# Layer 0's output projection in pairs of tiles by seven half-size block products, with the residual by accumulating DMAs, in a two-layer backbone

## The chip, the cores and the metric

The kernel runs on one core of one Trainium2 chip. The metric is the device time of one execution in microseconds (us). The engines are called PE (TensorE, matmuls), PEld (TensorE's weight load, which overlaps PE), DVE (VectorE), ACT (ScalarE), POOL (GpSimd) and SP (SyncE, which here issues DMAs only). Each of them works through its own queue of instructions in order; DMAs can be issued from SP, ACT and POOL. L1940 means line 1940 of the kernel before.

## The reference

A backbone of two layers over 2304 tokens (256 of a context, 2048 latent), 1024 wide. Each layer normalizes, modulates by a condition, mixes, projects, gates and adds the residual:

```python
for i in range(DEPTH):                       # DEPTH = 2
    shift, scale, gate = modulation(c, ada_w[i], ada_b[i])
    c_shift, c_scale, c_gate = modulation(c_ctx, ada_w[i], ada_b[i])
    h = rms_norm(x, norm_g[i]) * (1 + scale) + shift
    hc = rms_norm(cx, norm_g[i]) * (1 + c_scale) + c_shift
    if i % 2 == 0:
        y, yc = even_mixer(h, hc, ...)       # latent attention and gated linear attention, then @ ev_w_out
    else:
        y, yc = odd_mixer(h, hc, ...)        # neighbourhood attention, then @ od_w_out
    x = x + gate * y
    if update_ctx:                           # layer 0 only
        cx = cx + c_gate * yc
return x
```

What the change touches is the end of each layer. Layer 0: `x1 = xin + gate0 * (R @ w_out0)`, where `R` (2304x1024, kept transposed in device memory as `RT`) is the mixer's gated output, `w_out0` is 1024x1024, and the first two tiles of tokens, the context, take another gate vector. Layer 1: `out = x1 + gate1 * ((RT1 * z1) @ w_out1)` for the latent tokens alone, where `z1` is the mixer's own gate.

## The kernel before, in words

The tokens are 18 tiles of 128. All matmuls are single-precision by three products: each operand is split into a high part (a rounding, done by ACT at L106) and a low part (the difference, done by DVE), and `hi*hi + hi*lo + lo*hi` is accumulated in PSUM (L108 to L131; L129, L130 and L131 are the three).

The program is built under a scheduler that simulates the engines: it decides the order of the instructions in each engine's queue, and hoists an instruction as far as its inputs and its place in memory let it. `issue_after(x)` holds an instruction behind `x`. Buffers come from pools of named tiles; a load into a tile waits until its last user is done.

Stages, with their times in the profiled execution:

- *Constants, modulation and the latent products* (0 to 545 us). `ada_first` (L255, L258) multiplies the 8 MB of layer 0's modulation weights `ada_w` by the condition; `transposed` (L326) loads a tile, normalizes it (squares on ACT, the reciprocal root by `rpow`, L208 and L210, on POOL, the scaling at L336 on DVE) and transposes it on PE (L339, tile `px`); `modulate` makes `hhi` and `hlo` from it. Tile 0's `transposed` stands ahead of `ada_first`.
- *The rest of layer 0's input products*, `even_rest` (L607; 545 to 1095 us), cell by cell: for a tile and a column block, matmuls, an activation, and a store by a DMA from POOL (L635 to L639).
- *Mixing*, `even_mix` (L1164; 1095 to 1895 us): attention and the gated linear attention woven together; in it the 16 chunks of `w_out0` are split into high and low parts as room comes free (`unit`, L1210 ff.), and tile 0's load and split for the projection are made early.
- *Layer 0's output*, `project` (L1296; 1895 to 2093 us). For each of the 18 tiles: `project_load` (L1258) loads the tile of `RT` (`pr`, 512 KB) and the residual tile of the input (`px`, 512 KB) on SP; `project_split` (L1266; ACT L106, DVE L1268) makes its parts `prh` and `prl`; `project_steps` (L1270) runs two halves of 512 columns, each 8 blocks of k by three matmuls into a PSUM bank `pj`, multiplies a half by the gate into `py` (DVE, L1284), adds the residual (POOL, L1288) and stores the tile to `x1` (SP, L1290). 48 matmuls per tile, 864 in all. After each tile a step of `ahead()` runs: splits of layer 1's weight blocks `w_od` j = 2 and 3, and the preparation of layer 1's tiles 0 and 1 from `x1`.
- *Layer 1's input products*, `odd_qk` and `odd_vz` (2093 to 3010 us). The copies of `x1` into the output (L1455, 16 of 512 KB, ACT's queue, device memory to device memory) belong to `odd_vz` in the source; the scheduler has them at 1942 to 2098 us, each after the store of its tile.
- *Layer 1's attention and output* (3010 to 3567 us). The output is already done the new way: four plain tiles, then six pairs of tiles. A pair is a 2x2 block product (rows: two tiles; k and columns: halves of 512) by seven products of half size, 12 matmuls each, 84 in all, where two plain tiles take 96 (`seven`, L1920 ff.; the matmuls at L1940). It needs sums and differences of the weight blocks once (`weight_sums`, L1847), of the operands per pair (`operands`, L1910), copies of three partial results by ACT, and final sums and gates on DVE (L1950 ff.). The results are added to the output by accumulating DMAs from POOL (L1286 for plain tiles, L1960 for pairs, 256 KB each). The product with `z1` (`product`, L1808, 128x1024 elements) runs on POOL.

Of the kernel before, what the change touches and what calls it, by code (L numbers as in the profile page):

```python
# [17 lines left out]
P = 128  # L18
# [70 lines left out]
class Kern:  # L89
# [236 lines left out]
    def transposed(self, t, src, pp, tag, xp=None):  # L326

        nc, sp = self.nc, self.prp
        x = self.tl(xp or sp, [P, D], "x", bufs=1)
# [71 lines left out]
    def even_latent(self, ws, wrest, kept):  # L401
# [6 lines left out]
        with ExitStack() as es:  # L408
# [3 lines left out]
            with ExitStack() as es2:  # L412
                st = self.pool(es2, "adaS", side="left", reuse_waits="tile")
                rows = self.transposed(0, self.i["xin"], pp, px, st)
# [192 lines left out]
    def even_rest(self, ws, win, hT):  # L607
        nc = self.nc
        self.zaT = self.scr("zaT", (4, P, T), F32)
        with ExitStack() as es:  # L610
# [5 lines left out]
            def cell(t, j):  # L616
# [547 lines left out]
    def even_mix(self, e1, win, hT):  # L1164
        nc = self.nc
        self.RT = self.scr("RT", (KD, P, T), F32)
        self.x1 = self.scr("x1", (T, D), F32)
        with ExitStack() as es:
            with ExitStack() as esa:
# [31 lines left out]
                def side():  # L1201
# [11 lines left out]
                    pre[0] = self.project_load(self.RT, 0, self.i["xin"], ld)  # L1213
                    yield "unit"
                    yield "unit"
                    r, x = pre[0]
                    hi, lo = self.tl(ld, [P, KD, P], "prh", F32R, bufs=1), self.tl(ld, [P, KD, P], "px", F32R)
                    self.project_split(r[:], hi[:], lo[:])
                    pre[0] = hi, lo, r, x
# [9 lines left out]
            def ahead():  # L1229
                for j in (2, 3):  # L1230
                    yield from self.od_steps(win, j, ws)
                for t in range(2):
                    hT[t] = self.prep(1, t, self.x1, pp, ("pj", 4))
                    yield
                    yield

            u = 2 * KD - 1
            self.split_unit(w, u, self.load_unit(u, self.tl(sp, [P, 512], "py")), [self.tl(g1, [P, 512], "gG", F32R, bufs=2)[:] for _ in range(2)])
            gate = [self.gate_load(0, c, self.tl(sp, [P, D], f"gate{c}", bufs=1)[:]) for c in range(2)]
            self.project(self.RT, range(NT), self.i["xin"], self.x1, w, sp, pp, pre["ld"], pre, gate, ahead())  # L1240
# [17 lines left out]
    def project_load(self, RT, t, xsrc, ld):  # L1258
# [3 lines left out]
        x = self.tl(ld, [P, D], "px")  # L1262
        self.nc.sync.dma_start(x[:], xsrc[t * P : t * P + P, :])
        return r, x
# [26 lines left out]

    def gate_load(self, l, c, g):
# [3 lines left out]
    def project(self, RT, tiles, xsrc, dst, w, sp, pp, ld, pre, gate, ahead):  # L1296

        for t in tiles:
            if t in pre:
                hi, lo, r, x = pre.pop(t)  # L1300
            else:
                hi, lo = [self.tl(sp, [P, KD, P], "pr" + c, F32R)[:] for c in "hl"]
                r, x = self.project_load(RT, t, xsrc, ld)
                self.project_split(r[:], hi, lo)
            for _ in self.project_steps(hi, lo, x, gate[1 if t < NCT else 0], w, lambda: self.tl(pp, [P, 512], "pj", bufs=4),
                                        lambda: self.tl(sp, [P, 512], "py"), dst[t * P : t * P + P, :]):
                pass
            next(ahead, None)


# [212 lines left out]
    def odd_attention(self, out, right, left, wout):  # L1523
# [4 lines left out]
        with ExitStack() as es:  # L1528
# [278 lines left out]
            def product(z, r):  # L1807
                nc.gpsimd.tensor_tensor(out=r[:], in0=r[:], in1=z[:], op=ALU.mult)  # L1808
# [20 lines left out]
            PLAIN = 4  # L1829
            h4 = KD // 2  # L1830
            half = [slice(0, 512), slice(512, D)]
            by_k = lambda x: x.rearrange("p (k t) -> p k t", t=P)
            T1, T2, T3, T4 = [], [], [], [[x[:, 0, :] for x in wout[k, 1]] for k in range(h4)]
            B = lambda k0, n: [[x[:, 0, :] for x in wout[k, n]] for k in range(k0, k0 + h4)]

            def room():

                for dst, i in ((T1, 1), (T2, 0)):
                    q = [qtile(9, i, 1), qtile(9, i, 2)]
                    dst.extend([x[:, k * 512 : k * 512 + 512] for x in q] for k in range(h4))  # L1840
                v = self.tl(vp[1], [P, NT, P], "ov", F32R, bufs=1)[:].rearrange("p t d -> p (t d)")
                tb = [self.tl(tp[1], [P, NR, NC], f"tab{i}", F32R, bufs=1)[:].rearrange("p r c -> p (r c)") for i in range(2)]
                T3.extend([v[:, k * 512 : k * 512 + 512], tb[k // 2][:, k % 2 * 512 : k % 2 * 512 + 512]] for k in range(h4))

            def weight_sums():

                dif = lambda e, o, x, y: e.tensor_tensor(out=o, in0=x, in1=y, op=ALU.subtract)  # L1847
# [6 lines left out]
                room()  # L1854
                for k in range(h4):
                    u, v = [(low[i][:, half[0]], low[i][:, half[1]]) for i in (k, k + h4)]
                    dif(nc.vector, u[0], u[1], u[0])
                    self.project_split(u[0], *T1[k])
                    dif(nc.vector, u[1], v[1], u[1])
                    dif(nc.vector, v[1], v[1], u[0])  # L1860
                    self.project_split(v[1], *T2[k])
                    yield
                    dif(nc.vector, v[0], v[0], v[1])
                    self.project_split(u[1], *T3[k])
                    if k == h4 - 1:
                        late_sums.extend((low[i][:, half[0]], T4[i - h4]) for i in range(h4, KD))
                    yield

            late_sums = []
            sums_w = weight_sums()  # L1870
# [16 lines left out]
            def whole(x):  # L1887
                return by_k(x[:].rearrange("p i c -> p (i c)"))
# [4 lines left out]

            hA = [whole(self.tl(kp, [P, 2, 512], "kt1", F32R, bufs=2)) for _ in range(2)]
            h4w = whole(ones["kt"][1])
            hS4 = [h4w[:, :h4, :], h4w[:, h4:, :]]
            hS, hB = two(1), two(0)
            first4, last4 = slice(0, h4), slice(h4, KD)

            def pair_load(t):  # L1900

                za, ra = tile(t)
                zb, rb = tile(t + 1)
                product(za, ra)
                product(zb, rb)
                return za, ra, zb, rb

            def operands(za, ra, zb, rb):

                tt = lambda o, x, y, op: nc.vector.tensor_tensor(out=o, in0=x, in1=y, op=op)  # L1910

                def sums():
                    tt(za[:, first4, :], rb[:, first4, :], rb[:, last4, :], ALU.add)
                    tt(za[:, last4, :], za[:, first4, :], ra[:, first4, :], ALU.subtract)
                    self.project_split(za[:], *hS)

                def more():
                    tt(rb[:, first4, :], ra[:, first4, :], rb[:, first4, :], ALU.subtract)
                    tt(zb[:, first4, :], ra[:, last4, :], za[:, last4, :], ALU.subtract)
                    self.project_split(zb[:, first4, :], *hS4)  # L1920

                return [lambda: self.project_split(ra[:], *hA), sums, more, lambda: self.project_split(rb[:], *hB)]

            def seven(t):

                nonlocal mm, done
                end = t + 2 == NT - NCT
                if end:
                    res = exps([P, 512])
                    self.load(res[:], self.x1[CTX + (t + 1) * P : CTX + (t + 2) * P, :512])  # L1930
                U = self.tl(pp, [P, 8, 64], "o", bufs=4)[:].rearrange("p r c -> p (r c)")
                V, W = bank()[:], bank()[:]
                tile_of = lambda h, n: [x[:, n * h4 : n * h4 + h4, :] for x in h]

                def prod(ps, A, Bk, start):
                    nonlocal mm
                    with self.tc.issue_after(mm.ins) if mm else ExitStack():
                        for k in range(h4):
                            for n, (x, y) in enumerate(((A[0], Bk[k][0]), (A[0], Bk[k][1]), (A[1], Bk[k][0]))):
                                mm = nc.tensor.matmul(ps, x[:, k, :], y, start=start and k == 0 and n == 0, stop=k == h4 - 1 and n == 2,  # L1940
                                                      skip_group_check=True)

                def copy(ps, pool, tag, bufs):
                    x = self.tl(pool, [P, 512], tag, bufs=bufs)
# [158 lines left out]
```

## Time and profile before

| | us |
|---|---|
| median of 3 runs | 3563.45 (3563.01 to 3563.81) |
| profiled execution, its own time | 3569.04 |
| span of its trace | 3567.2 |
| PE busy in the span | 3465.4 (97%) |
| DVE, ACT, POOL busy | 2400.1, 1419.3, 1248.8 |
| mean granted clock of PE | 0.987 |

The span is the profiled execution's trace from its first to its last record; the 1.8 us around it are not in the trace. The *table of stretches* gives busy time by engine in chosen windows of the span; the *chain* follows the work that ended last back from the end, from each piece to what released it; a *timeline* lists one engine's instructions in order of start, with the idle time ahead of each and what ended it in brackets; a view *by tile* or *by line* lists the instructions that touch a tensor or stand on a line, as minimum, median and maximum duration. Busy time is no measure of what a stage costs: what matters is which engine is never idle in that stage, or which wait ends last.

### The profile page before, as it was taken

To read this page: it belongs to the slowest core of one execution; us is meant where nothing else is said; L and a number is where in the kernel's file an instruction comes from. 1 tells how busy PE (TensorE), PEld (TensorE's weight loads), DVE (VectorE), ACT (ScalarE), POOL (GpSimd) and SP (SyncE) were. 2 spreads that over 40 slices of the span, in tenths; PEclk is the share of its full clock that TensorE was granted. 3 is DMA by queue.
4 is the path that set the end of the run, shared out by engine and by line. 5 is a ranking of instruction groups with operands and counts; after the bars stand their busy time and mean duration, and the time that the engine had idled before them with its cause. 6 is when DMAs were issued, how large, how long until landed. Compare 5 with 4: busy or idle time off the path is not lost.

```text
span 3567.2 us, 54003 instructions
## 1 busy us (share of the span) xinstructions
PE 3465.4 (97%) x19532; PEld 2680.1 (75%) x19532; DVE 2400.1 (67%) x4709; ACT 1419.3 (40%) x2562; POOL 1248.8 (35%) x1382
## 2 busy tenths in 40 slices
PE   7999998999999999999999999999899999999999
PEld 6888987888896666665557878888788887555577
DVE  4677655888885777768874345545577784666775
ACT  5454552111113455446653124444422223555532
POOL 1333431100101333322212233333334443888842
PEclk9999999999999999999999999999999999999999
DMA  7555554222215242334526654445744447888675
GB/s 252 150 155 161 148 144 137 72 87 76 86 52 153 64 132 79 110 111 139 169 82 210 212 174 134 139 144 167 234 146 127 145 121 189 214 218 223 188 213 92
DMA packets 377292, 521.52 MB, mean 146 GB/s; under 512 B 34153, under 2 KB 253753, under 8 KB 370866
## 3 DMA queue, kind: packets, MB, share of 16 engines
q1 hardware_dynamic: 329762, 418.42, 40.7%
q0 software_dynamic: 24096, 63.26, 6.8%
q10 hardware_dynamic: 23168, 36.38, 2.9%
q8 instruction: 155, 2.54, 0.3%
q14 instruction: 111, 0.91, 0.1%
HBM read 338.62 MB, written 187.69 MB: 148 GB/s over the span
## 4 chain that ended last, share of the span: by engine, by line
PE 80%; DMA 7%; DVE 6%; ACT 2%; POOL 2%; issue 2%; SPq 1%; DVEq 0%; ACTq 0%; POOLq 0%
PE st L1130 10%; PE gm L129 10%; PE gm L130 10%; PE gm L131 10%; PE av L1040 7%; PE mx L660 4%; PE o L1624 2%; PE st L1590 2%; DMA wraw<-w_od 2%; PE pj L129 2%; PE pj L131 2%; PE pj L130 2%; PE o L1940 2%; DMA adaw<-ada_w 1%; PE st L1940 1%
## 5 line engine op out<-in xcount | busy, mean ns | idle before, releaser
L661 DVE TENSOR_REDUCE mm<-mx 128x1 f32<-128x512 f32 (+1 forms) x656 | 388.6, 629 | 82.3 <-PE mx L660 75.2
L106 ACT ACTIVATE apt<-st 128x1024 f32<-128x1024 f32 (+1 forms) x296 | 300.2, 1015 | 308.6 <-PE st L1130 293.7
L1137 DVE TENSOR_TENSOR acc<-acc,apt 128x1024 f32<-128x1024 f32 x256 | 340.6, 1330 | 81.0 <-ACT apt L106 61.6
L1130 PE MATMUL st<-aq,akh 64*128 64x512 f32 x1728 | 313.9, 410 | 1.1 <-ACT apt L106 0.8
L1040 PE MATMUL av<-apt,av 128*64 128x512 f32 x1152 | 265.8, 598 | 0.0
L1749 DVE TENSOR_TENSOR opt<-st,tab 128x64 f32<-128x64 f32 (+10 forms) x576 | 144.5, 318 | 144.3 <-PE st L1591 66.4
L660 PE MATMUL mx<-mk,mq 96*128 96x512 f32 (+1 forms) x656 | 236.0, 373 | 2.1 <-DMA mq<-QC 1.4
L1630 POOL TENSOR_TENSOR oacc<-oacc,opt 128x576 f32<-128x576 f32 (+5 forms) x192 | 223.3, 1190 | 38.5 <-DVE oacc L1614 13.8
L1130 PE MATMUL st<-aq,akl 64*128 64x512 f32 (+1 forms) x1152 | 231.8, 392 | 0.0
L1130 PEld LDWEIGHTS st<-aq,akh 64*128 64x128 f32 x1728 | 154.1, 186 | 83.0 <-ACT apt L106 29.1
L106 ACT ACTIVATE u<-gm 128x352 f32<-128x352 f32 (+1 forms) x140 | 68.5, 497 | 368.3 <-PE gm L131 208.3
L1507 DVE CUSTOM_DVE_ANT_1 mx<-mx,mtab 128x217 f32<-128x217 f32 (+12 forms) x576 | 184.0, 338 | 37.5 <-PE mx L1501 28.2
L1040 PEld LDWEIGHTS av<-apt,av 128*64 128x64 f32 x1152 | 76.3, 136 | 135.2 <-issue 134.2
L106 ACT ACTIVATE opt<-opt 128x930 f32<-128x930 f32 (+8 forms) x130 | 104.4, 805 | 110.0 <-DVE opt L1749 106.4
L660 PEld LDWEIGHTS mx<-mk,mq 96*128 96x128 f32 x656 | 121.2, 188 | 14.9 <-DVE mm L661 1.9
L1130 PEld LDWEIGHTS st<-aq,akl 64*128 64x128 f32 (+1 forms) x1152 | 113.0, 185 | 23.1
L106 ACT ACTIVATE x<-px,modB,modA 128x128 f32<-128x128 f32 x272 | 99.5, 468 | 59.5 <-PE px L339 56.5
L129 PE MATMUL gm<-w1h,hhi 128*128 128x512 f32 x288 | 116.2, 404 | 6.9 <-ACT onat L106 6.9
L129 PE MATMUL gm<-w0h,hhi 128*128 128x512 f32 x288 | 116.5, 404 | 1.9 <-DVE hhi L351 1.9
L130 PE MATMUL gm<-w1l,hhi 128*128 128x512 f32 x288 | 115.1, 400 | 0.0
L210 POOL TENSOR_TENSOR oss<-oss,mhalf 128x8 f32<-128x8 f32 x68 | 113.2, 1665 | 5.1
L130 PE MATMUL gm<-w0l,hhi 128*128 128x512 f32 x288 | 114.6, 398 | 0.0
(579 smaller groups left out, 9700.9 us busy)
## 6 DMA issues: line engine op xcount, KB each, us to landing
q<-Q SPq DMA_DIRECT2D x48, 512.0 KB
H<-x ACTq DMA_DIRECT2D x36, 512.0 KB
adaw<-ada_w SPq DMA_DIRECT2D x64, 256.0 KB
x<-H SPq DMA_DIRECT2D x32, 512.0 KB
wraw<-w_od SPq DMA_DIRECT2D x64, 256.0 KB
K1t<-okt POOLq DMA_DIRECT2D x32, 512.0 KB, 7.3
kt<-K1t SPq DMA_DIRECT2D x32, 512.0 KB
mtab<-rpb_q SPq DMA_DIRECT2D x16, 899.0 KB
```

Of the source, the lines that this page charges most:

```text
L106: return self.nc.scalar.activation(out, in_, func, **kw)
L129: self.nc.tensor.matmul(out, lh(k), rh(k), start=start and j == 0, stop=False)
L130: self.nc.tensor.matmul(out, lh(k), rl(k), start=False, stop=False)
L131: yield self.nc.tensor.matmul(out, ll(k), rh(k), start=False, stop=stop and j == n - 1)
L660: mm = nc.tensor.matmul(ps[:, :w], q[:A_QK, (t % 6) * P : (t % 6) * P + P], k[:A_QK, k0 : k0 + w], start=True, stop=True)
L661: nc.vector.tensor_reduce(out=m[:, t, n : n + 1], in_=ps[:, :w], axis=AX.X, op=ALU.max)
L1040: mm = nc.tensor.matmul(O[j, nb][i * 64 : i * 64 + 64, :w], V[j, kt // TT][:, kt % TT, i * 64 : i * 64 + 64], pts[:, i, :w], start=n == 0, ...
L1130: mm = nc.tensor.matmul(ps[:, o // 64, :w], k[o : o + r, kb, kq], Q[o : o + r, qb, :w], start=m == 0, stop=m == 4)
L1137: added = nc.vector.tensor_tensor(out=acc[:, :, :w], in0=a[:, :, :w], in1=pts[:, :, :w], op=ALU.add)
L1507: nc.vector.tensor_tensor_reduce(out=s, in0=s, in1=tb[:, ri : ri + rn, ci : ci + cn], scale=1.0, scalar=-3e38, op0=ALU.add, op1=ALU.max, a ...
L1630: self.psum = nc.gpsimd.tensor_tensor(out=a, in0=a, in1=pts[:, :, a0 - r0 : a1 - r0, :], op=ALU.add)
L1749: bias = nc.vector.tensor_tensor(out=pt[:, d[0], d[1]], in0=ps[:, d[0], d[1]], in1=tabs[j][i][:, ri : ri + rn, ci : ci + cn], op=ALU.add)
```

## The change

1. Layer 0's output: tiles 0 to 3 stay plain; tiles 4 to 17 are taken in seven pairs, each by seven block products (780 matmuls in all instead of 864). The code of layer 1's pairs becomes shared methods (`weight_sums`, `pair_operands`, `seven`, `pair_result`).
2. The residual: in `even_rest`, behind the cell j = 1 of each tile, a DMA from POOL copies the tile of the input to `x1`, in device memory (18 of 512 KB). The results are added to `x1` by accumulating DMAs from POOL of 256 KB (two per plain tile, four per pair: 36). The loads of `px`, POOL's adds and the stores of `x1` go.
3. The rest of the weight sums' operands are loaded as whole rows of `w_out0` (8 of 512 KB on SP) at the stage's start, and the sums are made during the plain tiles.
4. The splits of `w_od` j = 2 move into the pairs, those of j = 3 to the end of the last pair (their place holds two weight sums until then); layer 1's tiles 0 and 1 are prepared inside the last pair.
5. Layer 1's product with `z1` moves from POOL to DVE.

The core of the diff:

```diff
 def even_rest(self, ws, win, hT):
+    self.x1 = self.scr("x1", (T, D), F32)
...
             elif j == 1:
                 nc.gpsimd.dma_start(self.Un[t, :, 1056:], u[:])
+                nc.gpsimd.dma_start(self.x1[t * P : t * P + P, :], self.i["xin"][t * P : t * P + P, :])
...
 def even_mix(self, e1, win, hT):
-    self.x1 = self.scr("x1", (T, D), F32)
...
-        self.project(self.RT, range(NT), self.i["xin"], self.x1, w, sp, pp, pre["ld"], pre, gate, ahead())
+        self.even_output(w, sp, pp, pre, win, hT, ws)
...
+    def seven(self, h, w, U, V, W, copy, result):
...
+        prod(U, part(h["A"], 0), w["B11"], True)
+        s1 = copy(U, 0)
+        prod(V, part(h["S"], 0), w["T1"], True)
+        s5 = copy(V, 1)
+        prod(U, part(h["S"], 1), w["T2"], False)
+        u2 = copy(U, 2)
+        prod(W, part(h["A"], 1), w["B21"], True)
+        self.done = result(W, s1, 0, 0)
+        yield
+        prod(U, part(h["B"], 0), w["T3"], False)
+        self.done = result(U, s5, 1, 1)
+        yield
+        prod(V, h["S4"], w["B22"], False)
+        self.done = result(V, u2, 0, 1)
+        yield
+        prod(U, part(h["B"], 1), w["T4"], False)
+        self.done = result(U, None, 1, 0)
+        yield
...
+    def even_output(self, w, sp, pp, pre, win, hT, ws):
...
+        def weights7():
+            raw = [self.tl(ws[0], [P, h4, D], "w0" + z, bufs=1) for z in "hl"]
+            for k in range(h4):
+                for n, x in enumerate(raw):
+                    nc.sync.dma_start(x[:, k, :], self.i["w_out0"][:, n * h4 + k, :])
...
+            for k in range(h4):
+                yield from self.weight_sums(raw[0][:, k, :], raw[1][:, k, :], *(w7[t][k] for t in ("T1", "T2", "T3")))
+            late.extend((raw[1][:, k, self.HALF[0]], w7["T4"][k]) for k in range(h4))
...
+        def result(t):
+            def f(ps, x, row, n):
+                x, done = self.pair_result(ps, x, gates[0][:, self.HALF[n]], y)
+                nc.gpsimd.dma_start(self.x1[(t + row) * P : (t + row) * P + P, self.HALF[n]], x[:], accum_op=ALU.add)
+                return done
+            return f
...
+        ahead = self.od_steps(win, 2, ws)
+        for t in range(PLAIN, NT, 2):
+            end = t + 2 == NT
+            if not end:
+                ops = pair(t + 2)
+            U = self.tl(pp, [P, 512], "pu", bufs=2)
+            for n, _ in enumerate(self.seven(h7, w7, U[:], bank()[:], bank()[:], copy, result(t))):
+                if not end:
+                    with self.tc.issue_after(self.done.ins):
+                        ops[n]()
+                    if n == 3:
+                        next(ahead, None)
+                elif n < 2:
+                    xp = None if n == 0 else (ld, "pr")
+                    hT[n] = self.modulate(1, n, *self.transposed(n, self.x1, pp, ("pj", 4), xp))
+        for _ in ahead:
+            pass
+        for _ in self.od_steps(win, 3, ws):
+            pass
...
             def product(z, r):
-                nc.gpsimd.tensor_tensor(out=r[:], in0=r[:], in1=z[:], op=ALU.mult)
+                nc.vector.tensor_tensor(out=r[:], in0=r[:], in1=z[:], op=ALU.mult)
```

More of the change, by code (lines that the diff above doesn't have):

```diff
@@ L1299, in project @@
             if t in pre:
[L1300 removed]
+                hi, lo = pre.pop(t)
             else:
[L1302 to L1307, printed above, removed]
@@ L1308, in project @@
-            next(ahead, None)
+                hi, lo = parts()
+                self.project_split(self.project_load(self.RT, t, ld)[:], hi, lo)
+            if t == 0:
+                next(sums)
+            for n, _ in enumerate(self.project_steps(hi, lo, None, gates[1 if t < NCT else 0], w, bank, y, self.x1[t * P : t * P + P, :])):
+                if t and n % 5 == 4:
+                    next(sums, None)
+        for _ in sums:
+            pass
+        s4 = self.tl(ld, [P, KD, P], "prh", F32R, bufs=1)
@@ new lines, in even_output @@
+        ops, self.mm = pair(PLAIN), None
+        for n in range(4):
+            ops[n]()
+            if n == 1:
+                for x, place in late:
+                    self.project_split(x, *place)
+        ahead = self.od_steps(win, 2, ws)
[7 more added lines that the diff above has]
+                    with self.tc.issue_after(self.done.ins):
+                        ops[n]()
+                    if n == 3:
[3 more added lines that the diff above has]
+                    hT[n] = self.modulate(1, n, *self.transposed(n, self.x1, pp, ("pj", 4), xp))
@@ L1892, in two @@
                 return [by_k(x[:, i].rearrange("p r c -> p (r c)")) for i in range(2)]
[L1894 to L1903, printed above, removed]
+            s4 = whole(ones["kt"][1])
@@ L1904, in pair_load, with pair @@
+            h7 = {"A": [whole(self.tl(kp, [P, 2, 512], "kt1", F32R, bufs=2)) for _ in range(2)], "S": two(1), "B": two(0),
+                  "S4": [s4[:, :h4, :], s4[:, h4:, :]]}
+            def pair(t):
+                (za, ra), (zb, rb) = [tile(t + n) for n in range(2)]
                 product(za, ra)
                 product(zb, rb)
[L1906 to L1922, printed above, removed]
@@ L1981, in odd_attention, with copy, result, f @@
-            after = pair_load(PLAIN)
-            ops, done = operands(*after), None
+                return self.pair_operands(ra[:], rb[:], za[:], h7)
+            def copy(ps, n):
+                x = self.tl(fp, [P, 512], "rc", bufs=3) if n == 2 else self.tl(lp, [P, 512], "rl", bufs=2)
+                self.act(x[:], ps)
+                return x
+            def result(t, res):
+                def f(ps, x, row, n):
+                    add = x is None and res
+                    x, done = self.pair_result(ps, x, gate[:, self.HALF[n]], y)
+                    dst = out[(t + row) * P : (t + row) * P + P, self.HALF[n]]
+                    if add:
+                        nc.vector.tensor_tensor(out=x[:], in0=x[:], in1=res[:], op=ALU.add)
+                        nc.sync.dma_start(dst, x[:])
+                    else:
+                        nc.gpsimd.dma_start(dst, x[:], accum_op=ALU.add)
+                    return done
+                return f
@@ L1988, in odd_attention @@
             for t in range(PLAIN, NT - NCT, 2):
-                if t + 2 < NT - NCT:
-                    after = pair_load(t + 2)
-                    ops = operands(*after)
-                for n, _ in enumerate(seven(t)):
-                    if t + 2 < NT - NCT:
-                        with self.tc.issue_after(done.ins):
+                end = t + 2 == NT - NCT
+                if not end:
+                    ops = pair(t + 2)
+                else:
+                    res = exps([P, 512])
+                    self.load(res[:], self.x1[CTX + (t + 1) * P : CTX + (t + 2) * P, :512])
+                U = self.tl(pp, [P, 8, 64], "o", bufs=4)[:].rearrange("p r c -> p (r c)")
+                for n, _ in enumerate(self.seven(h7, w7, U, bank()[:], bank()[:], copy, result(t, res))):
+                    if not end:
+                        with self.tc.issue_after(self.done.ins):
                             ops[n]()
```

194 lines of the change are left out of this document (92 added, 102 removed).

## The prediction

> **What bounds the kernel now.** I read the page first (busy time, slices, chain), then the table of stretches stage by stage, then the timelines of the engines in the stretches that the change touches.
>
> ```profile
> span 3567.2 us, 54003 instructions
> PE 3465.4 (97%) x19532; PEld 2680.1 (75%) x19532; DVE 2400.1 (67%) x4709; ACT 1419.3 (40%) x2562; POOL 1248.8 (35%) x1382
> PE 80%; DMA 7%; DVE 6%; ACT 2%; POOL 2%; issue 2%; SPq 1%; DVEq 0%; ACTq 0%; POOLq 0%
> 0.00:5.00 5.00, 0.00 (x0) 0.00 (x0) 0.69 (x4) 1.50 (x2) 1.40 (x12) 1.00 0.41 121
> 10.00:15.00 5.00, 4.68 (x18) 1.48 (x16) 0.00 (x0) 0.00 (x0) 0.00 (x0) 1.00 1.00 424
> 25.00:30.00 5.00, 4.24 (x24) 2.03 (x24) 1.29 (x3) 1.77 (x4) 0.00 (x0) 1.00 1.01 396
> 40.00:100.00 60.00, 49.35 (x282) 46.13 (x282) 38.18 (x56) 30.61 (x67) 10.99 (x18) 0.94 0.60 186
> 100.00:545.00 445.00, 428.30 (x2570) 394.71 (x2570) 305.21 (x574) 229.10 (x538) 167.41 (x307) 0.99 0.56 151
> 1970.00:2090.00 120.00, 120.00 (x538) 99.45 (x538) 43.47 (x41) 17.35 (x28) 29.97 (x24) 1.00 0.58 195
> ```
>
> TensorE (PE) is busy 97% of the span and is 80% of the chain, so a matmul that goes is worth its time wherever PE is full. The rows of stretches give, after the length, the busy time of PE, PEld, DVE, ACT and POOL, then granted clock, DMA share and GB/s. Layer 0's output (1895 to 2093 us) is a stage in which PE is never idle and the other engines are under half busy. The start is the opposite: from 10 to 30 us the sixteen DMA engines are full (share 1.00, about 424 GB/s).
>
> **The change, part by part.** All sums are differences, first against the profiled execution (3569.04 us, span 3567.2), which is 5.59 above the median of the runs, 3563.45; I add the sum to the median.
>
> *1. The products.* Seven pairs take 84 matmuls where two plain tiles take 96.
>
> ```profile
> 2009.74 0.39 PE L129 MATMUL pj<-D,prh 128*128 128x512 f32 x1
> 2009.97 0.39 PE L130 MATMUL pj<-D,prh 128*128 128x512 f32 x1
> 1955.35 0.69 DVE L1284 TENSOR_TENSOR py<-pj,gate 128x512 f32<-128x512 f32 x1 [2.02 <-PE pj L131]
> 1960.79 0.69 DVE L1284 TENSOR_TENSOR py<-pj,gate 128x512 f32<-128x512 f32 x1 [4.75 <-PE pj L131]
> 3484.16 2.79 PE st L1940 x12
> 3503.62 2.79 PE st L1940 x12
> 3523.08 2.79 PE st L1940 x12
> 3542.54 2.79 PE st L1940 x12
> ```
>
> A half tile (24 matmuls) ends every 5.44 us by the DVE rows, 0.227 per matmul; two tiles are 4 x 5.44 = 21.76 us. A pair by seven products exists in layer 1: the chain's rows repeat every 19.46 us. At the plain pitch it would be 84 x 0.2267 = 19.04. So a pair saves 2.30 to 2.72, seven pairs **16.1 to 19.0 us; I take 17.5**, between the two because this stage ran at clock 1.00, layer 1's at 0.98. Weight sums (28 DVE operations of 128x512, 0.69 each, 19 us) and T4's splits lie beside the four plain tiles (44 us, in which DVE is a third busy); the loads of tiles 1 to 3 stand ahead of the 4 MB of weights on SP, so none of it costs PE time. POOL's adds and the stores were not on the path: nothing is gained from them.
>
> *2. The residual copies.* In the source they stand in the second stage (545 to 1095 us). But nothing that they read is produced by the kernel, and in the built program's order for POOL all 18 stand at the very start, right behind the constants: eight without a wait, the next eight each waiting for the copy eight before it, then the first half of tile 0's root-mean-square (L208), then copies 17 and 18 (waiting for 9 and 10), then its second half (L210). Two things are queued behind a wait there: tile 0's normalization, and through it every first product. And 9.44 MB travel in the stretch whose DMA engines are full.
>
> ```profile
> 4.51 15.89 DMA adaw<-ada_w
> 27.14 3.61 PE gm L258 x16
> 35.39 0.94 PE L120 MATMUL gm<-W0h,hhi 128*128 128x352 f32 x2
> 2087.08 0.50 ACTq L1455 DMA_DIRECT2D out_dram<-x  x1
> 2088.00:2089.00 1.00, 1.00 (x6) 0.84 (x5) 0.48 (x1) 0.00 (x0) 0.44 (x1) 1.00 1.37 459
> 2089.00:2090.00 1.00, 1.00 (x6) 0.82 (x5) 0.00 (x0) 0.00 (x0) 0.85 (x1) 1.00 0.16 66
> 6.60 0.19 POOL L208 TENSOR_SCALAR ssx<-ssx 128x1 f32<-128x1 f32 x1 [4.62 <-ACT hlo L106]
> 6.88 0.58 POOL L210 TENSOR_TENSOR ssx<-ssx,mhalf 128x1 f32<-128x1 f32 x1
> q1 hardware_dynamic: 3996, 12.74, 75.7%
> q10 hardware_dynamic: 100, 1.67, 10.9%
> ```
>
> The chain begins with the 8 MB of modulation weights, which the first weight product (35.39) waits for. A copy DRAM to DRAM of 512 KB, alone, held the engines for 1.37 + 0.16 = 1.53 engine-us: 18 of them are 27.5 us by that, and 9.44 MB at the 424 GB/s of the full stretch are 22.3 us. [...] Least: nothing, if PE's idle time behind (10.65 us from 40 to 100, 16.7 from 100 to 545) takes all of it up; most: 27.5. **I take +21**, near the row of the full stretch. Afterwards PE is 96% busy to 545 us and 99% to 1095, so little is regained.
>
> [...]
>
> *3. Waits in the pairs.* Results now leave by accumulating DMAs, and copies of x1 to the output, issued on ACT's queue, wait for their landing.
>
> ```profile
> L1960 POOL DMA_DIRECT2D out_dram<-rl x12: 859/869/1185, 3458.8 to 3555.5; - x12
> DMA to landing us min/median/max: 3.6/4.3/8.8
> 3455.00:3465.00 10.00, 6.85 (x27) 4.97 (x26) 9.93 (x11) 3.23 (x4) 6.67 (x6) 0.95 0.66 111
> ```
>
> In the first pair, the output copy of tile 2 stands on ACT ahead of the late weight splits, B's split, two splits of the next stage's weights and the copy of U that frees the bank for product 3. Tile 2's DMAs are issued before tile 3's 10.9 us, so most of the 0.87 + 4.3 is over, but tile 3's copy stands ahead of V's copy and is issued at the moment the pair begins. I charge **+4.4** (0 to +7): one landing (4.3), about the stall layer 1 shows where its first pair starts (3.15 us of PE in ten). In each later pair the previous pair's last result must land before ACT takes this pair's second copy of U; it has two products (5.6 us) for 0.87 + 4.3, so the median fits and a slow landing (8.8) does not: **+1.5** over six pairs (0 to +7).
>
> *4. Into layer 1.* The output copies of the last pair and w_od j=3, now split only at the end, stand on ACT ahead of tile 2's preparation.
>
> ```profile
> 2119.40 1.94 PE L339 MATMUL px<-ident,x 128*128 128x128 f32 x8 [3.38 <-DVE x L336]
> 2115.00:2140.00 25.00, 21.10 (x92) 17.01 (x91) 11.67 (x20) 10.70 (x24) 13.77 (x21) 0.86 0.63 191
> ```
>
> PE already waits 3.38 us here; by my count of what ACT has ahead (eleven weight chunks) tile 2 comes 2.4 us later: **+2.4** (0 to +5).
>
> *5. Layer 1's product on VectorE.*
>
> ```profile
> L1808 POOL TENSOR_TENSOR opt<-opt,opt x15: 2372/2405/3433, 3385.9 to 3507.5; 128x1024 f32<-128x1024 f32 x15
> 3405.00:3435.00 30.00, 29.01 (x124) 22.83 (x123) 30.00 (x39) 9.52 (x14) 11.99 (x9) 1.00 0.67 165
> 3426.78 3.34 DVE kt L1268
> 3465.00:3540.00 75.00, 75.00 (x319) 60.43 (x319) 45.44 (x58) 20.10 (x26) 25.95 (x20) 0.98 0.61 121
> ```
>
> DVE is full from 3405 to 3435, where PE is nearly full too. A product would cost DVE about 1.23 (the 128x1024 rows of DVE), but while POOL makes one, DVE operations of 0.60 or 0.69 last up to 3.34; the stretch can as well get shorter. From 3465 on PE is full and nothing changes. The prize is the first pair's 3.15 and some 3 us of short waits before it: **-3** (-6 to +2).
>
> Sum: -17.5 + 21 + 4.4 + 1.5 + 2.4 - 3 = **+8.8 us**; 3563.45 + 8.8 = 3572.3. With the bounds of all terms at once it runs from -25 to +32.4.
>
> **Rivals.** *(a) The delay at the start is taken up behind it* (faster). If the 27 us in which PE is idle up to 545 are waits for work that is not delayed, the copies cost only some 3 us. For it: the DMA engines have 40% to spare from 40 us on. Against: the chain there is itself weight loads and their splits, which shift with the start. Price: the other terms sum to -12.2, so the copies decide: under 12.2 us of delay left, the change is faster, under 5.1 clearly so. With 3 left: 3554.3. *(b) The landing waits stall every pair.* If a landing takes 8.8 (the slowest row) instead of 4.3, each of six pairs waits 0.87 + 8.8 - 5.6 = 4.1 us, 24 in place of 1.5: 3595. For it: copies of 512 KB and weight loads share the engines there (share 0.58 to 0.87). Against: the median. *(c) The change doesn't do what it says*: the pairs gain nothing because the operand sums (about 12 us of DVE per pair) hold PE. Then -17.5 is 0 and the time 3590. Layer 1's pairs, with the same sums, ran PE full; this is unlikely.
>
> **How the numbers follow.** Forecast 0.55 (3562 to 3583), (a) 0.25, (b) 0.15, (c) 0.05. The range takes in most of (a) and half of the way to (b): 3551 to 3590. About 0.2% (7.1 us) is what a measurement of this kernel can tell from no change. Faster than 3556.3: most of (a) and a little of the forecast, 0.28; within: the rest of (a) and the forecast's lower part, 0.22; slower than 3570.6: the forecast's larger part, (b) and (c), 0.50.
>
> **What would show it.** Step 2: the x1 copies at 2 to 30 us in POOL's timeline, DMA share at 1.0 until about 50, and the first weight product near 56 instead of 35.39; the stage ends shifted by the same. Step 1: the DVE rows of a pair 19.0 to 19.5 us apart. Step 3: a PE wait of 4 or 5 us for ACT in the first pair, short or none later. Step 4: the wait before px of tile 2 at 5 to 6. Step 5: no DVE operation of 2 to 3 us after 3400 and a shorter stall at the first pair. I am wrong if the first weight product starts before 44 us, if the shift at 545 us is under half of that at 35, or if pairs repeat at over 20.5 us.

## The result, and the profile after

The changed kernel is slower: 3605.49 us (median of 4 runs, 3597.36 to 3610.96) against 3563.63 for the kernel before in the same runs, a ratio of 1.0113 with a 95% interval of 1.0091 to 1.0135. The forecast was 3572.3, in a range up to 3590. The profiled execution took 3602.51 us, its span is 33.5 us longer than before's. The medians lie 41.9 us apart: the profiled execution of before took 5.4 us more than the median of its runs here, that of the change 3.0 less. Part of before's 5.4 may lie in the last stretch but one of the table below (first to last wide product of layer 1's attention): 353.6 us, the longest in the fourteen traces (344.7 to 352.6 in the others). The page after:

```profile
span 3600.7 us, 53999 instructions
PE 3462.6 (96%) x19448; PEld 2672.9 (74%) x19448; DVE 2451.9 (68%) x4819; ACT 1452.4 (40%) x2613; POOL 1203.9 (33%) x1385
PE   5999998999999999999999989999899999999999
```

84 matmuls are gone (19448 instead of 19532), and PE is not busier, but the slices show what took their place: the first holds 5 tenths (7 before), and the 24th, in which layer 1 begins, 8 (9 before). I followed one first instruction through both traces, stage by stage:

| instruction | before | after | later by |
|---|---|---|---|
| first weight product of layer 0 (L120) | 35.39 | 66.30 | 30.9 |
| first product of the second stage's maxima (L660 before) | 564.8 | 598.1 | 33.3 |
| first product of the projection's second weight place | 1898.2 | 1926.9 | 28.7 |
| first product of layer 1's block j = 0 (`w2h`) | 2135.6 | 2168.3 | 32.7 |
| first product of layer 1's maxima (`mx<-mk,mz`) | 2564.7 | 2595.5 | 30.8 |
| first wide product of layer 1's attention | 3013.4 | 3048.9 | 35.5 |
| last of these | 3367.0 | 3398.1 | 31.1 |
| span | 3567.2 | 3600.7 | 33.5 |

So the whole loss is there at 565 us, 4.6 us of it come back by the projection, and the projection, which was to gain, ends with the step into layer 1 4 us worse than it began. The rows of these two places follow. First the start, stretches of the changed kernel and PE's timeline (in brackets the idle time before an instruction, and what ended it):

```profile
10.00:40.00 30.00, 11.64 (x32) 3.34 (x32) 0.86 (x2) 0.60 (x1) 4.84 (x11) 0.77 1.00 377
50.00:55.00 5.00, 4.24 (x24) 1.88 (x22) 1.26 (x3) 0.60 (x1) 0.00 (x0) 1.00 1.01 396
```

```profile
15.43 3.68 PE L258 MATMUL gm<-adaw,cond 128*64 128x512 f32 x8 [15.43 <-DMA adaw<-ada_w]
25.24 3.68 PE L258 MATMUL gm<-adaw,cond 128*64 128x512 f32 x8 [6.13 <-DMA adaw<-ada_w]
33.71 3.30 PE L258 MATMUL gm<-adaw,cond 128*64 128x512 f32 x8 [4.79 <-DMA adaw<-ada_w]
41.81 3.68 PE L258 MATMUL gm<-adaw,cond 128*64 128x512 f32 x8 [3.81 <-DMA adaw<-ada_w]
57.66 1.05 PE L264 MATMUL up<-adasel,adarow 128*128 128x2 f32 x8 [0.76 <-ACT adarow L106]
66.30 0.95 PE L120 MATMUL gm<-W0h,hhi 128*128 128x352 f32 x2 [3.36 <-ACT W0h L106]
```

The DMA engines are full until 55 us instead of 30 (share 1.00 and 1.01 in the rows), and PE waits for `ada_w` four times. The rows of PE before, for comparison:

```profile
20.53 1.94 PE L258 MATMUL gm<-adaw,cond 128*64 128x512 f32 x8 [0.28 <-DMA adaw<-ada_w]
31.48 1.05 PE L264 MATMUL up<-adasel,adarow 128*128 128x2 f32 x8 [0.76 <-ACT adarow L106]
```

The last small product of the modulation (L264) starts at 57.66; before it was 31.48, so the modulation, which needs all of these loads, came **26.2 us** later. Part of this may be PE's own pace: eight products between two waits last 3.68 us, 1.94 before. The granted clock is 0.77 from 10 to 40 us, but in e2 below it is 1.00 in the same stretch, and eight such products last 3.68 us there too (at 33.68 us). How much of the 26.2 us the pace makes is not separated. From L264 to the first weight product were 3.9 us before and are 8.6 now. On ACT, tile 1's modulation now stands ahead of the split of the first weights (W0h):

```profile
62.12 2.91 ACT L106 ACTIVATE x<-px,modB,modA 128x128 f32<-128x128 f32 x8 [0.72 <-PE px L340]
65.45 2.84 ACT L106 ACTIVATE W0h<-adaw 128x704 fp32r<-128x704 f32 x4 [0.42 <-ACT x L106]
```

The step into layer 1, PE's timeline and stretches of the changed kernel:

```profile
1977.03 1.22 PE L1323 MATMUL pu<-w1h,prh 128*128 128x512 f32 x2 [3.89 <-ACT py L106]
2102.95 0.72 PE L1323 MATMUL pu<-w1l,prh 128*128 128x512 f32 x2 [0.87 <-ACT py L106]
2132.49 1.12 PE L1503 MATMUL tp<-ident,onat 128*128 128x128 f32 x4 [4.97 <-DVE onat L1495]
2150.14 1.09 PE L1503 MATMUL tp<-ident,onat 128*128 128x128 f32 x4 [8.12 <-DVE onat L1495]
2154.51 0.79 PE L129 MATMUL gm<-w0h,hhi 128*128 128x512 f32 x1 [1.23 <-DVE hhi L352]
```

```profile
1972.00:1985.00 13.00, 9.11 (x30) 6.95 (x29) 6.22 (x9) 4.69 (x9) 0.86 (x1) 0.74 0.80 223
2000.00:2090.00 90.00, 90.00 (x393) 73.33 (x392) 52.74 (x72) 24.77 (x32) 16.39 (x19) 1.00 0.74 166
2140.00:2160.00 20.00, 10.57 (x37) 8.01 (x36) 11.88 (x19) 10.36 (x21) 12.76 (x18) 0.66 0.87 253
```

Between the first pair and the last PE is never idle: the pairs run as they should. PE waits 3.9 us in the first pair, 0.9 in the last and 14.3 us in the step (3.9 before). In the first pair it waits for the copy of U (`py<-pu`), and on ACT that copy stands behind splits of layer 1's weights `w_od` that wait for their loads:

```profile
1974.61 0.63 ACT L106 ACTIVATE w0h<-wraw 128x512 fp32r<-128x512 f32 x1 [3.50 <-DMA wraw<-w_od]
1975.86 0.63 ACT L106 ACTIVATE w0h<-wraw 128x512 fp32r<-128x512 f32 x1 [0.62 <-DMA wraw<-w_od]
1976.40 0.58 ACT L106 ACTIVATE py<-pu 128x512 f32<-128x512 f32 x1
```

### The profile page after: what moved, and what is told of

Same layout as the page of the kernel before. It is cut to its first block, busy times and chain, and to the rows that moved or that the text cites. A ratio compares the mean times of both kernels' runs of the same rounds, so it can differ in the third digit from the quotient of the medians.

```text
span 3600.7 us, 53999 instructions
## 1 busy us (share of the span) xinstructions
PE 3462.6 (96%) x19448; PEld 2672.9 (74%) x19448; DVE 2451.9 (68%) x4819; ACT 1452.4 (40%) x2613; POOL 1203.9 (33%) x1385
## 3 DMA queue, kind: packets, MB, share of 16 engines
q8 instruction: 154, 2.52, 0.3%
## 5 line engine op out<-in xcount | busy, mean ns | idle before, releaser
L131 PE MATMUL gm<-w0h,hlo 128*128 128x512 f32 x288 | 114.6, 398 | 0.0
```

Of the source, the lines that this page charges most:

```text
L131: yield self.nc.tensor.matmul(out, ll(k), rh(k), start=False, stop=stop and j == n - 1)
```

## The experiments

Every kernel was compared with the kernel before, run beside it; ratios are to that. "Held" means that an instruction is tied behind another (`issue_after`), so that the scheduler cannot hoist it.

**e1, the copies into x1 held** behind their tile's store, on the changed kernel:

```diff
-                    nc.gpsimd.dma_start(self.Un[t, :, 1056:], u[:])
-                    nc.gpsimd.dma_start(self.x1[t * P : t * P + P, :], self.i["xin"][t * P : t * P + P, :])
+                    st = nc.gpsimd.dma_start(self.Un[t, :, 1056:], u[:])
+                    with self.tc.issue_after(st.ins):
+                        nc.gpsimd.dma_start(self.x1[t * P : t * P + P, :], self.i["xin"][t * P : t * P + P, :])
```

> The changed kernel, but each of the 18 copies into x1 held behind its tile's store in the second stage, so that none stands at the program's start. If the copies at the start are the cause of the start's 33 us (engines shared by bytes, POOL's queue, and the order that follows), the first weight product is back at about 35 us, the shift at the first max product (564.8 us before) is 0 to 2 us, and the time is 3605 - 31 = about 3574. If the later losses (transition, layer 1) are knock-ons of the late start, they go too and the time is about 3556. If the copies only move their cost into the second stage, the shift at 1095 us stays at 10 or more.

3583.63 us, 1.0053 (1.0036 to 1.0070): 22 us less than the change, not 31. The start is as expected (first product of the maxima at 568.7, 3.9 later than before). But the later losses did not go: PE waits 8.10, 8.11 and 1.25 us in the step. So they are no knock-on of the start. The rest is no clean subtraction: from 565 us to the projection this kernel loses 2.3 us where the change won 4.6, and in the step it waits 17.5 us where the change waits 14.3; why is open.

**e2, the copies alone**, in the kernel before, into a place that nobody reads (`+ nc.gpsimd.dma_start(self.xd[...], self.i["xin"][...])` behind the same store):

> The kernel before with nothing added but 18 copies of 512 KB from the input to an unused place in device memory, issued from POOL as in the change (the scheduler puts them at the start in the same order). If the copies alone make the start late, the first weight product is at about 66 us and the time 3563.6 + 31 to 33 = about 3595. If the late start comes from the rest of the change (another order of the transposes through the scheduler's plan), it is within 5 us of before.

3596.81 us, 1.0092 (1.0077 to 1.0107), 32.5 us over before; the first weight product:

```profile
67.34 0.95 PE L120 MATMUL gm<-W0h,hhi 128*128 128x352 f32 x2 [3.38 <-ACT W0h L106]
```

The copies by themselves make the start late, and all of it stays to the end.

**e7, 18 tiny copies** (one row of 4 KB each) and **e8, 9 of the 18 copies**, in the kernel before:

> The kernel before with 18 copies from POOL as in the kernel with copies alone, each of one row (4 KB instead of 512 KB). If the bytes make the start late, the first weight product is at 35 to 37 us. If the 18 issues on POOL ahead of tile 0's normalization or the order of the transposes do, it stays at 50 or later.

> The kernel before with 9 of the 18 copies of 512 KB. By bytes at the full stretch's rate (424 GB/s) the first weight product comes 11 us later than before, 46 to 47 us; if the 18 copies' 31 us are a fixed part for the order on the queues (some 9) and the rest bytes, 20 us later, 55.

e7 took 3566.13 us, 1.0002 (0.9992 to 1.0013), e8 3582.36, 1.0049 (1.0033 to 1.0065). In e8's timeline:

```profile
45.13 1.05 PE L264 MATMUL up<-adasel,adarow 128*128 128x2 f32 x8 [0.76 <-ACT adarow L106]
53.45 0.96 PE L120 MATMUL gm<-W0h,hhi 128*128 128x352 f32 x2 [3.68 <-ACT W0h L106]
```

In e7 the first weight product stands at 35.41 us: the 18 issues on POOL, and the other place of tile 0's transposes (23.22 us, 8.30 before), cost nothing; the bytes do (67.34 in e2). The modulation comes 45.13 - 31.48 = 13.65 us later with 9 copies and 26.2 with 18, that is 1.52 and 1.46 us per copy. From there to the first weight product it is 8.3 us in e8 and 8.6 in the change, 3.9 before: a fixed part of 4.5 us. e8's first product lay 18 us later, between its two expectations: bytes in proportion, and a fixed part half as large as I had thought.

**e3, also the copies of x1 into the output held** behind the activation that they follow in the source:

```diff
-                self.act(z[:], pt[:])
+                za = self.act(z[:], pt[:])
...
-                    nc.scalar.dma_start(self.out[o : o + P, :], self.x1[CTX + o : CTX + o + P, :])
+                    with self.tc.issue_after(za.ins):
+                        nc.scalar.dma_start(self.out[o : o + P, :], self.x1[CTX + o : CTX + o + P, :])
```

> As the copies-held kernel, and the copies of x1 into the output held behind the activation that they follow in the source (third quarter of the kernel), so that none stands on ACT during layer 0's output and the step into layer 1. If the waits of ACT for landings cause the first pair's 3.9 us and the step's 10.4 us of extra PE idle time, the time is 12 to 14 us under that of the copies-held kernel (about 3561). If the late split of the w_od blocks by itself causes the step's loss, only 2 to 5 us go.

3567.60 us, 1.0010 (1.0001 to 1.0020), 15 us below e1 by the ratios: the size expected, but not from the place expected. The step still waits:

```profile
2106.14 1.12 PE L1504 MATMUL tp<-ident,onat 128*128 128x128 f32 x4 [7.44 <-DVE onat L1496]
2121.21 1.09 PE L1504 MATMUL tp<-ident,onat 128*128 128x128 f32 x4 [5.52 <-DVE onat L1496]
2125.21 0.79 PE L129 MATMUL gm<-w0h,hhi 128*128 128x512 f32 x1 [1.21 <-DVE hhi L352]
```

14.2 us against 17.5 in e1, and the first pair 2.4 against 3.2. From the projection to the block j = 0, e1 loses 8.5 us and e3 1.3, the pairs' gain included; from the layer-1 maxima to its attention e1 loses 7.7 us and e3 1.5. The first of these, 7.2 us, bounds from above what the output copies cost there: the change itself, with the copies on ACT, waits 14.3 us in the step and takes only 2.7 us more than e3 over the same stretch. Whether it is their landings on ACT or their bytes is not separated. The second is not shown to be theirs: e9 below, with these copies held, loses 8.8 us there too. Another 3.2 us of e3's 15 lie ahead of 565 us, where the two kernels do the same.

What PE waits for in the step is seen on ACT. This is e3's timeline of ACT:

```profile
2092.42 0.63 ACT L106 ACTIVATE w1h<-wraw 128x512 fp32r<-128x512 f32 x1 [6.65 <-DMA wraw<-w_od]
2094.44 0.63 ACT L106 ACTIVATE w1h<-wraw 128x512 fp32r<-128x512 f32 x1 [1.38 <-DMA wraw<-w_od]
...
2098.53 0.63 ACT L106 ACTIVATE w2h<-wraw 128x512 fp32r<-128x512 f32 x1 [1.45 <-DMA wraw<-w_od]
2099.99 0.63 ACT L106 ACTIVATE w2h<-wraw 128x512 fp32r<-128x512 f32 x1 [0.83 <-DMA wraw<-w_od]
2100.52 0.58 ACT L106 ACTIVATE osq<-gm 128x512 f32<-128x512 f32 x1
```

PE waits for `onat`, that for the squares `osq`, and they stand on ACT behind splits of w_od j = 3 and j = 0 that each wait for their load, about one per 1.5 us. Before, j = 3 had been split at 1921 to 1938 us beside the plain tiles; now its place holds the weight sums T2 and T3 until the last pair, and 24 chunks instead of 16 pass through three staging buffers in the step.

**e6, the splits of j = 0 and 1 held behind tile 2's squares**, on e3; **e11, the same hold alone**, on the change as it was:

```diff
-            self.ahead += [self.od_steps(win, 0, ws), self.od_steps(win, 1, ws)]
+            self.sqs.clear()
+            self.ahead += [self.behind(self.od_steps(win, j, ws), 2) for j in (0, 1)]
```

(`behind` gives out a step under `issue_after` of the activation with which `transposed` squares that tile, here tile 2.)

> The kernel with both kinds of copies held, and the splits of w_od j = 0 and 1 held behind the squares of tile 2, so that on ACT the squares of the first cells and of tile 2 no longer stand behind splits that wait for loads. If the order on ACT is what makes PE wait in the step, the step's 14 us of idle time fall to 6 or less and the time is 3567.6 - 8 to 10 = 3558 to 3560, faster than before. If it is the loads' own rate (three buffers of 256 KB), the wait only moves to the first use of j = 0 and the time stays within 3 us of 3567.6.

> The change as it was measured, with only the splits of w_od j = 0 and 1 held behind tile 2's squares; the copies at the start and the output copies on ACT stay. If the order on ACT in the step is a cause of its own, 7 to 11 us go from 3605.5 (3595 to 3598) although the rest is as before; if it needed the output copies to be away from ACT, less than 4 go.

e6: 3556.64 us, **0.9975 (0.9965 to 0.9985)**, 12 us below e3 by the ratios and faster than before. Its step:

```profile
2100.73 0.66 PE L1517 MATMUL tp<-ident,onat 128*128 128x128 f32 x4 [0.78 <-DVE onat L1509]
2111.69 1.09 PE L1517 MATMUL tp<-ident,onat 128*128 128x128 f32 x4 [2.97 <-DVE onat L1509]
2116.95 0.50 PE L129 MATMUL gm<-w0h,hhi 128*128 128x512 f32 x1 [2.47 <-DVE hhi L364]
```

6.2 us of waits instead of 14.2, and PE does not wait at the first product of j = 0 (2130.1 us): the order on ACT was the main cause, not the rate of the loads. e11: 3588.68 us, 1.0073 (1.0057 to 1.0089), 14 us below the change by the ratios (17 by the medians), more than expected: the cause stands by itself, with the other copies still in place. Between the projection and the block j = 0, where the hold acts, the traces give 12.0 us from e3 to e6 and 9.3 from the change to e11.

**e5, j = 3 split late in the kernel before** (taken out of `ahead()`, and stepped through behind the last tile):

> The kernel before, with the splits of w_od j = 3 taken out of the work beside the projection's tiles and made behind its last tile, as in the change; nothing else. If the late j = 3 (24 chunks of weights in the step into layer 1 instead of 16, through three staging buffers, with ACT's and DVE's other work queued behind splits that wait for their loads) causes the step's loss, PE's idle time in the step rises from 3.9 us to 12 to 16 and the time is 8 to 14 us above before. If the loss comes from the pairs (accumulating DMAs, tiles 0 and 1 prepared inside the last pair), it is within 3 us of before.

3565.72 us, 0.9998 (0.9988 to 1.0007). This tells nothing of the question: the scheduler put the splits back where they were (1921.9 to 1937.9 us), since nothing in that kernel holds their place. That a late j = 3 makes the step wait in a kernel with plain tiles stays untested.

**e10, the kernel before with both holds** (output copies, splits of j = 0 and 1):

> The kernel before with the output copies and the splits of w_od j = 0 and 1 held in the same two ways; plain tiles, no pairs in layer 0. If the gain of the held kernel over before comes from the pairs, this one is within 3 us of before. If it comes from the two holds, which also cure something in the kernel before (3.4 us of PE idle time at tile 2), it is 4 us or more below.

3567.27 us, 1.0016 (1.0006 to 1.0026). The holds by themselves gain nothing, so what e6 gains over before comes from the change's own work: 0.9975 / 1.0016 is 0.41% or 15 us, close to the pairs' 16.9 us below.

**e4, layer 1's product on DVE in the kernel before; e9, the product back on POOL in e6:**

> The kernel before with layer 1's product (15 operations of 128x1024) on DVE. If the products stand on DVE ahead of results that PE waits for (the changed kernel's 4.4 us stall), the time is 1 to 4 us above before. If they only take away the slow operations beside POOL, as the prediction had it, it is 3 us below.

> The kernel with the copies and the splits held, and layer 1's product back on POOL. If the product on DVE is worth something (the prediction's 3 us), the time is 2 to 4 us above 3556.6; if it only exchanges one stall at the first pairs for another (3.3 + 2.0 us of PE idle time against 3.2 before), it is within 2 us.

e4: 3563.02 us, 0.9994 (0.9984 to 1.0003); e9: 3555.85, 0.9980 (0.9970 to 0.9990). Neither shows a difference clear of the noise, but e4's interval (5.7 us less to 1.1 more) does not exclude the 3 us of the forecast. The stalls change their place. In the changed kernel's tail, DVE and then PE:

```profile
3478.81 1.23 DVE L1946 TENSOR_TENSOR opt<-opt,opt 128x1024 f32<-128x1024 f32 x1 [2.43 <-DMA opt<-RT]
3481.89 1.23 DVE L1946 TENSOR_TENSOR opt<-opt,opt 128x1024 f32<-128x1024 f32 x1 [1.85 <-DMA opt<-RT]
3484.90 1.23 DVE L1946 TENSOR_TENSOR opt<-opt,opt 128x1024 f32<-128x1024 f32 x1 [1.79 <-DMA opt<-RT]
```

```profile
3491.87 0.79 PE L1323 MATMUL o<-wo0h,oacc 128*128 128x512 f32 x1 [4.40 <-DVE rl L1349]
```

The slow DVE operations beside POOL's products are gone: in the kernel before, seven operations of 128x512 lasted 1.90 to 2.89 us and two of 128x1024 3.11 and 3.42 between 3417 and 3498 us, each beside a product on POOL; in the changed kernel, from 3419 us on, they last 0.67 to 0.70 and 1.22 or 1.23. Ahead of that, beside POOL's accumulations (`oacc`), some slow ones remain, the first product on DVE among them (2.52 us, at 3415.54). But the products stand in DVE's queue and wait there for their loads, ahead of the results of the first pair (L1349), which PE waits for.

**e12, the copies into x1 two cells earlier** (behind cell j = 4), on e6:

> The kernel with all held, but the copies into x1 behind the store of cell j = 4 instead of j = 1, two cells (some 10 us) earlier for each tile. The first 100 us of the mixing stage had 94.3 us of PE busy time with the copies held at j = 1, 96.0 before: if the last copies are in the way of the stores that this stage loads, 2 to 4 us go (3553 to 3555); if not, it stays at 3556.6.

3560.91 us, 0.9997 (0.9987 to 1.0007), slower than e6. The first 100 us of mixing hold 95.4 us of PE work (94.3 in e6), but the time from the first max product to the last grew to 524.8 us (521.6 in e6). The expectation fell. Before, that time was 522.1 us, so the stage itself shows no cost of the copies in e6 and 2.7 us in e12; where the rest of e12's 8 us (by the ratios) lies is open.

## Why the prediction was wrong, step by step

The direction was right and the largest term named the right mechanism; the time lay 15 us above the range. The copies (step 2) cost more than charged, the mechanism of the step into layer 1 (step 4) was missed, and no run shows the gain of step 5.

*Step 1, the pairs (-17.5): right.* The gated results of the pairs repeat every 19.35 us, against 21.76 for two plain tiles: 2.41 each, 16.9 in seven.

```profile
2043.25 0.69 DVE L1349 TENSOR_TENSOR py<-pj,py 128x512 f32<-128x512 f32 x1 [7.75 <-issue]
2062.60 0.69 DVE L1349 TENSOR_TENSOR py<-pj,py 128x512 f32<-128x512 f32 x1 [7.75 <-issue]
```

*Step 2, the copies (+21): the mechanism was right, the term mis-sized.* It measured 33.3 at the second stage (e2: 30.7 there, 32.5 in the time). Two parts were left out. The copies cost 1.46 us each, near the 1.53 engine-us of the row that I had quoted and set as the upper end, and not the 1.24 of the full stretch's rate; I chose the wrong one of two rows. And 4.5 us come from behind the loads, where the split of the first weights now comes last on ACT; why the scheduler put it there is not shown. The last 2 us or so, between the first weight product and 565 us, are in the change alone and stay open. Rival (a), that the idle time behind would take the delay up, is refuted by e2: the first weight product came 32 us later, and the time is 32.5 longer.

That the copies would come ahead of the loads was my estimate. In the first 45 us of the changed kernel, the DMA queues (packets, MB, share of the engines) are

```profile
q0 software_dynamic: 576, 9.44, 53.5%
q1 hardware_dynamic: 1387, 6.54, 40.7%
```

all 9.44 MB of the copies, in pieces of 16.4 KB, with the larger share of the engines and ahead of SP's last loads (q1 has moved 6.54 MB by 45 us, 11.63 by 60). In the kernel before, the first 45 us held SP's loads in pieces of 3.2 KB (the q1 row in step 2 of the prediction), and from 2060 to 2100 us the output copies came in pieces of 16.7 KB (its q10 row). So the copies and the loads shared the engines; why the copies had the larger share is not shown. e2 agrees on what they cost.

*Step 3, waits in the pairs (+4.4 and +1.5): the number about right, for the first pair by luck.* 3.9 us of idle time in the first pair, 0.9 in the last, none between. I had charged the first pair one landing of an output copy. But the copy of U waited behind splits whose loads came late, and in e3, which has no output copy on ACT here, most of the wait is still there, on ACT and on PE:

```profile
1948.28 1.25 ACT L106 ACTIVATE w0h<-wraw 128x512 fp32r<-128x512 f32 x2 [5.27 <-DMA wraw<-w_od]
1950.07 1.22 PE L1324 MATMUL pu<-w1h,prh 128*128 128x512 f32 x2 [2.41 <-ACT py L106]
```

So it is step 4's mechanism again. What I left out is the clock: the stretch of the first pair's wait was granted 0.74.

*Step 4, into layer 1 (+2.4): this step failed.* I had the right instructions in the right queue and gave them their own durations. Eight of the eleven chunks ahead of tile 2 (ACT, 2124 to 2142 us) waited for their load, and the squares of the first cells (`osq`), not only tile 2's preparation, stood behind them. It measured 14.3 - 3.9 = 10.4 us of idle time, and the granted clock was 0.66 from 2140 to 2160 us. From the projection's start to the block j = 0, idle time explains -16.9 + 4.8 + 10.4 = -1.7 us of the +4.0 in the table. The other 5.7 are busy time of PE, by the stretches of before, the change and e11:

```profile
1898.20:2135.60 237.40, 233.50 (x1035) 192.76 (x1034) 96.85 (x116) 54.09 (x90) 68.67 (x66) 0.99 0.66 217
1926.90:2168.30 241.40, 222.24 (x952) 180.48 (x951) 144.22 (x209) 87.16 (x141) 51.01 (x65) 0.95 0.76 194
1930.00:2162.10 232.10, 218.32 (x953) 177.41 (x952) 143.28 (x208) 86.14 (x140) 52.07 (x66) 0.98 0.77 199
```

233.5 less the pairs' 16.9 would be 216.6, and the change has 222.2. I put this down to the clock (0.95 instead of 0.99), an estimate: 216.6 x 0.99 / 0.95 would be 225.7. e11 supports it: with as many matmuls and shorter waits, PE is busy 3.9 us less than in the change, at a clock of 0.98. e6 and e11 show that the order is the cause: 12 and 14 us by one hold.

What lowers the clock is not shown. The stretches with waits of 3.9 and 8.1 us were granted 0.74 and 0.66, and e11, with waits of 1.8 to 3.6 us in the step, 0.98 over its stretch; but e2 was granted 1.00 from 10 to 40 us, where PE was busy for only 12.34 of the 30.

*Step 5, the product on DVE (-3): no gain shown.* The slow operations that I saw were real (up to 2.89 us for 128x512, 3.42 for 128x1024), and from 3419 us on they went (0.70 and 1.23). But in the changed kernel PE's last wait at the first pairs is for results that stand on DVE behind products waiting for their loads, and neither e4 nor e9 shows a difference clear of the noise.

Rival (b), landings that stall every pair, did not occur: between the first pair and the last PE is never idle. The forecast's sum of +8.8 missed 12 us at the start and some 8 to 14 in the step, was given 3 at the end that no run shows, and did not have the 4.6 us that came back ahead of the projection. With the busy time counted (14 in the step) these make up the 33.5 us between the two traces; the 8 us more between the medians belong to no step that the traces show.

## What to carry to other kernels

Before a DMA is priced where the source has it, look where the built order puts it: one that reads only inputs can go to the very start, as these did (1.9 to 26.1 us), where the loads that everything waited for already filled the engines (share 1.00 from 10 to 30 us). A split that waits for a load was not priced here by its own duration (0.63 us) but by the pace of the loads (about one per 1.5 us in e3's step), and all that stood behind it in its engine's queue paid too; one dependency that keeps urgent small work ahead of it was worth 12 to 14 us here. The pairs themselves were good: with the copies and splits held the same change is 0.25% faster than before.

## What the runs showed of the hardware that had not been expected

Copies of 512 KB within device memory delayed the modulation, which waits for the loads beside them, by 1.46 (18 copies, the change) to 1.52 us each (9 copies, e8), more than their bytes at the 424 GB/s that the loads alone reached from 10 to 15 us in the kernel before (1.24 us); together the two streams moved 377 GB/s from 10 to 40 us of the changed kernel. And 18 issues of tiny copies on POOL cost the start nothing (e7: first weight product at 35.41, before 35.39), although tile 0's transposes came at 23.22 us instead of 8.30.
